# Gate weights loaded earlier, two-chunk steps, and a first tile by pieces in a two-layer encoder trunk

## The chip, the cores and the metric

The kernel runs on one core of a Trainium2 chip. The metric is the device time of one execution in microseconds (us). Before the change the median of three runs is 2396.72 us, the lowest 2395.23 and the highest 2396.8.

## The reference

A trunk of two layers works on h, the 256 tokens with 16 learned meta tokens in front: 272 rows of 2048 numbers. Each layer does the following, in float32:

```
proj = h @ w_in            # GLA q, k, v, output gate r, low-rank decay lr; NA q, k, v
g    = log_sigmoid(lr @ w_up + b_up) / 16        # for each of two directions, 4 heads x 128
o    = gla_scan(q, k, v, g_fwd) + flip(gla_scan(flip q, flip k, flip v, flip g_bwd))
o    = o * rsqrt(mean(o^2) + eps) * norm_w * silu(r)      # heads of 256 value columns
y    = neighbourhood attention of 16 heads over a 4 x 64 grid, plus the meta tokens as keys
h    = layer_norm(alpha * h + concat(o, y) @ w_out)
h    = layer_norm(alpha * h + relu(h @ w_ff1)^2 @ w_ff2)
```

w_ff1 and w_ff2 have 8192 hidden columns. The meta rows are dropped from the output, which is 256 x 2048.

## The kernel before

**Weights.** All large products use float32 split in two: a high part rounded to the fast type fp32r, and a low part, the rest. A weight tile is 128 x 1024 (512 KB): SP loads it raw (L150), ScalarE casts it to wh (L151), VectorE subtracts to get wl (L152). Each of raw, wh and wl is a ring of three buffers, and `weights` makes two tiles ahead of the one in use. TensorE runs 24 matmuls with a tile (wh with the high and the low part of x, wl with the high part; where only 256 rows are wanted, one matmul of 512 columns takes both parts of x). The activations x, y and u lie in SBUF as pairs (high, low), 16 pairs each, as places of a fixed name (y0 to y15).

**Loops.** `by_m` (L203) makes one output chunk of 128 columns after the other, with all of its weight tiles, through `eight` (L157). `by_k` (L183) keeps four accumulators (eight where `wide`) and goes through the inner chunks two at a time; it starts the kernel, where x arrives chunk by chunk (`load_x`, L304), and starts other stages whose inputs become ready one after the other. PSUM has four banks "mm" for the accumulators and four banks "bg" for everything else.

**Background work.** Everything beside the large products is written as generators whose steps are put between the weight tiles. `pump` (L105) runs so many steps of the queue fg and of the queue bg after each tile. In the queue fg of each layer stand first `gates` (L334), then for each of the eight value chunks `v_rows` (L388), which transposes a chunk of v into rows, splits it into high and low and stacks the meta rows. `gla_head` (in bg) does the attention of a head; its output is two chunks, each with seven matmuls on its own bank (L569 to L581), one step each. Each engine carries out its instructions in order, so a waiting instruction holds up all behind it on that engine; a step is put behind the newest weight split (`issue_after`, L99).

**Gates.** `gates` loads wup (98 x 1024) into a place of its own and, a step later, wlr (128 x 512) into a buffer of the raw ring; in layer 0 it also loads the constants (L339). It then casts and splits both (L345, L348 to L350), makes lr with 32 small matmuls, and does eight steps, one for each head and direction: a matmul (L368), four activations (L370, L371, L372, L374) and one VectorE operation (L373). In layer 1 it is queued after the first `by_m` and `by_k` have been written out (L263), when the places of the layer before have been closed.

**First tile.** `load_x` loads the first x chunk (L313), and `made` loads the first weight tile in pieces of 256, 256 and 512 columns; after the first piece it loads the second x chunk (L154). The 24 matmuls go through the products with wh first, then those with wl (L196).

**The end.** `ln_out` (L953) normalizes the last layer per token. It transposes the accumulated chunks into eight blocks of 128 x 512 on eight banks (`turn`), sums with matmuls against ones (L979, L983), casts the mean and its low part for a matmul that centres the blocks (L985, L986, `centre`), makes the variance (L989, L990), takes two further steps for the root (`newton`, L450 to L454), and scales each block by it with the bias added (L999 to L1002) before its output transfer (L1003).

## Time and profile before

| what | value |
|---|---|
| median of three runs | 2396.72 us |
| profiled execution, its own time | 2396.73 us |
| its span in the profile | 2394.9 us |
| TensorE busy | 2385.1 us (100%) |
| weight loads of TensorE busy | 2264.0 us (95%) |
| VectorE busy | 1539.6 us (64%) |
| ScalarE busy | 1216.7 us (51%) |
| GpSimd busy | 131.9 us (6%) |
| moved by DMA | 419.07 MB, mean 175 GB/s |
| weight splits L151, L152 | 770 of each, 1047 and 1225 ns |

How to read it: the span runs from the first to the last instruction of the profiled execution; its own time is a little longer. The page has the engines as PE and PEld (TensorE's matmuls and weight loads), ACT (ScalarE), DVE (VectorE), POOL (GpSimd) and SP (SyncE, which issues transfers here). A row of the timeline has the start, the time from the start to the end, the engine, the line, the operation with its output and inputs, the shape, how many such instructions stand in one row, and in brackets the idle time of the engine before it and what ended it. Matmuls overlap, so the time of one to the start of the next is shorter than its own. A row of the waits has who waited for whom, the sum in us, how often, and the longest. A row of windows has the stretch, its length, the busy share and number of instructions of TensorE, its weight loads, VectorE, ScalarE and GpSimd, the clock granted, the share of the DMA engines, and GB/s.

### The profile page before, as it was taken

The numbers are of one execution on the slowest core, as the hardware profiler recorded it, in microseconds if no ns is written. First come the engines' busy times: TensorE is split into PE (matmuls) and PEld (weight loads), VectorE is DVE, ScalarE is ACT, GpSimd is POOL, SyncE is SP. The second block draws the span as 40 slices with busy tenths as digits, with TensorE's granted clock in tenths as the row PEclk, the third lists the DMA queues.
The fourth block names the chain that finished last, engine by engine and source line by source line (L and its number), as shares of the span: only waits on it lengthen the run. The fifth ranks groups of instructions, "written<-read, shape, count | busy, mean of one in ns | idle before, by whom it ended". The sixth has DMA issues, their size and how long they took to land.

```text
span 2394.9 us, 43606 instructions
## 1 busy us (share of the span) xinstructions
PE 2385.1 (100%) x17666; PEld 2264.0 (95%) x17666; DVE 1539.6 (64%) x2473; ACT 1216.7 (51%) x2064; POOL 131.9 (6%) x202
## 2 busy tenths in 40 slices
PE   9999999999999999999999999999999999999999
PEld 9999999999999999999999999999988888888888
DVE  5598777775544455546576887778866445666654
ACT  5765655564433344444456766655644333444443
POOL 0021110010000000000021111100100000000000
PEclk9999999999999999999999999999999999999999
DMA  7444445555555555555556444446566555566654
GB/s 259 151 153 152 145 139 165 176 173 172 176 176 176 175 171 175 175 176 171 175 177 180 159 148 159 153 159 194 187 187 190 186 189 188 186 189 210 195 187 146
DMA packets 118073, 419.07 MB, mean 175 GB/s; under 512 B 13484, under 2 KB 14252, under 8 KB 117872
## 3 DMA queue, kind: packets, MB, share of 16 engines
q1 hardware_dynamic: 117584, 415.77, 54.9%
q8 instruction: 138, 2.26, 0.4%
q14 instruction: 63, 0.52, 0.1%
q10 hardware_dynamic: 288, 0.52, 0.1%
HBM read 414.14 MB, written 2.10 MB: 174 GB/s over the span
## 4 chain that ended last, share of the span: by engine, by line
PE 97%; DVE 1%; DMA 1%; ACT 1%; issue 0%; POOL 0%; SPq 0%; DVEq 0%; ACTq 0%; POOLq 0%
PE mm L169 35%; PE mm L172 29%; PE mm L166 23%; PE mm L199 5%; PE bg L199 1%; PE bg L504 1%; PE bg L684 1%; PE bg L633 1%; DVE wl L152 0%; PE bg L356 0%; DMA raw<-in_win 0%; PE bg L669 0%; DVE acc L913 0%; ACT wh L151 0%; POOL acc L901 0%
## 5 line engine op out<-in xcount | busy, mean ns | idle before, releaser
L152 DVE TENSOR_TENSOR wl<-raw,wh 128x1024 fp32r<-128x1024 f32 (+1 forms) x770 | 942.8, 1225 | 648.1 <-ACT wh L151 643.2
L151 ACT CAST wh<-raw 128x1024 fp32r<-128x1024 f32 (+1 forms) x770 | 805.6, 1047 | 950.7 <-PE mm L169 437.3
L169 PE MATMUL mm<-x,wh 128*128 128x272 f32 (+2 forms) x4224 | 582.0, 290 | 0.0
L169 PEld LDWEIGHTS mm<-x,wh 128*128 128x128 f32 x4224 | 548.3, 189 | 2.5 <-issue 1.1
L172 PE MATMUL mm<-x,wl 128*128 128x272 f32 (+3 forms) x3264 | 467.3, 285 | 0.0
L172 PEld LDWEIGHTS mm<-x,wl 128*128 128x128 f32 x3264 | 437.6, 188 | 13.1
L166 PE MATMUL mm<-x,wh 128*128 128x512 f32 x1152 | 294.3, 397 | 1.9 <-ACT ft L385 1.9
L166 PEld LDWEIGHTS mm<-x,wh 128*128 128x128 f32 x1152 | 207.7, 189 | 42.0 <-ACT ft L385 2.2
L172 PE MATMUL mm<-y,wl 128*128 128x272 f32 (+1 forms) x1408 | 199.5, 284 | 0.0
L172 PEld LDWEIGHTS mm<-y,wl 128*128 128x128 f32 x1408 | 188.9, 188 | 7.5
L169 PE MATMUL mm<-y,wh 128*128 128x272 f32 (+1 forms) x1440 | 195.8, 288 | 0.0
L169 PEld LDWEIGHTS mm<-y,wh 128*128 128x128 f32 x1440 | 186.1, 188 | 0.0
L166 PE MATMUL mm<-y,wh 128*128 128x512 f32 x688 | 174.1, 395 | 0.0
L172 PE MATMUL mm<-u,wl 128*128 128x272 f32 (+1 forms) x1024 | 145.3, 284 | 0.0
L166 PEld LDWEIGHTS mm<-y,wh 128*128 128x128 f32 x688 | 123.4, 188 | 22.5
L169 PE MATMUL mm<-u,wh 128*128 128x272 f32 (+1 forms) x1056 | 143.2, 288 | 0.0
L172 PEld LDWEIGHTS mm<-u,wl 128*128 128x128 f32 x1024 | 137.8, 188 | 5.6
L169 PEld LDWEIGHTS mm<-u,wh 128*128 128x128 f32 x1056 | 136.3, 188 | 0.0
L166 PE MATMUL mm<-u,wh 128*128 128x512 f32 x496 | 125.3, 395 | 0.0
L166 PEld LDWEIGHTS mm<-u,wh 128*128 128x128 f32 x496 | 89.1, 188 | 16.4
L199 PE MATMUL mm<-x,wh 128*128 128x272 f32 (+1 forms) x512 | 73.7, 289 | 0.5 <-ACT wh L151 0.4
L199 PEld LDWEIGHTS mm<-x,wh 128*128 128x128 f32 x512 | 68.0, 191 | 1.1 <-ACT wh L151 1.1
(261 smaller groups left out, 1886.4 us busy)
## 6 DMA issues: line engine op xcount, KB each, us to landing
raw<-in_wff SPq DMA_DIRECT2D x512, 512.0 KB, 3.6
raw<-in_win SPq DMA_DIRECT2D x191, 512.0 KB, 3.6
raw<-in_wout SPq DMA_DIRECT2D x64, 512.0 KB, 3.6
nb<-in_nab SPq DMA_DIRECT2D x16, 352.0 KB, 3.6
xraw<-in_xT SPq DMA_DIRECT2D x7, 272.0 KB, 5.7
out<-out SPq DMA_DIRECT2D x6, 256.0 KB, 3.0
brow<-in_norm SPq DMA_DIRECT2D x4, 256.0 KB, 5.0
wraw<-in_wup SPq DMA_DIRECT2D x2, 392.0 KB
```

The costliest lines, as they stand in the source:

```text
L151: nc.scalar.copy(wh[:, c], raw[:, c])
L152: self.wl = nc.vector.tensor_tensor(wl[:, c], raw[:, c], wh[:, c].bitcast(F32), ALU.subtract).ins
L166: mm(ps, lhsT=c(wh, j), rhs=v.both[:, :, :T], start=first and not j, stop=False)
L169: mm(ps[:, :n], lhsT=c(wh, j), rhs=v[i][:, :n], start=first and not i + j, stop=False)
L172: mm(o, lhsT=c(wl, j), rhs=h[:, :T if once else n], start=False, stop=last and j == 7)
L199: self.nc.tensor.matmul(ps[g + m][:, :n], lhsT=parts[p][0][:, c:c + P], rhs=acts[k + j][parts[p][1]][:, :n], start=k + j + p == 0, stop=k ...
L504: nc.tensor.matmul(ps[b * 64:b * 64 + 64, i * P + s * 64:i * P + s * 64 + 64], lhsT=k[:, c:c + 64], rhs=q[:, r:r + 64], start=True, stop=True)
L633: nc.tensor.matmul(ps[hh][:, t * NKEY:t * NKEY + NKEY], lhsT=q[hs, NM + t * P:NM + t * P + P], rhs=k[hs, t, :], start=True, stop=True)
L684: nc.tensor.matmul(r[hs], lhsT=(v2 if rest else v1)[:, t, hs], rhs=p2[:, t, :] if rest else p1[:, 2 * t + hh, :], start=rest, stop=not rest)
```

## The change

The change has six parts.

1. *First tile.* The second x chunk is loaded after the second piece of the weight tile instead of after the first, and the 24 matmuls of the first tile go by inner chunk and then by pairs of outputs, each pair with all three products.
2. *Gate weights.* A new function `load_gates` loads wup in two tiles of 98 x 512 and wlr in one of 128 x 512 into the places y8, y9 and y10. In layer 1 it is called when the layer begins, in layer 0 in the first step of `gates`. The cast and split of wup go in two pieces. wlr no longer takes a buffer of the raw ring.
3. *Gates.* One step does both directions of a head: two matmuls into two banks, two Abs of 272 columns, then Exp, Ln and Exp over both (544 columns), and two VectorE operations. There are four steps instead of eight in each layer.
4. *Value rows.* One generator does two chunks: six transposes in one step, then the splits and stacks of one chunk, a step's end, and those of the other.
5. *Outputs of a head.* The fourteen matmuls of both chunks are in one step.
6. *The end.* The per-token sums of the mean come before the matmul that spreads it; the mean is copied and squared by VectorE, no longer squared by ScalarE, and the variance is written ahead of mu; the first output block is scaled and sent in two halves of 256 columns, so that SP sends seven transfers instead of six.

The number of matmuls of each kind stays.

```diff
@@ -150,7 +150,7 @@
             nc.sync.dma_start(raw[:, c], ap[:, c])
             nc.scalar.copy(wh[:, c], raw[:, c])
             self.wl = nc.vector.tensor_tensor(wl[:, c], raw[:, c], wh[:, c].bitcast(F32), ALU.subtract).ins
-            if between and not p:
+            if between and p == 1:
                 between()
         return wh, wl
 
@@ -193,7 +193,7 @@
                 parts = ((wh, 0), (wh, 1), (wl, 0))
                 order = [(j, p, m) for j in range(2) for p in range(3) for m in range(4)]
                 by_output = k == nk - 2 or k == 0 and not wide
-                order.sort(key=lambda o: (by_output and o[2], o[1] // 2))
+                order.sort(key=lambda o: (o[0], o[2] // 2) if wide and not k + g else (by_output and o[2], o[1] // 2))
                 for j, p, m in order:
                     c = j * 512 + m * P
                     self.nc.tensor.matmul(ps[g + m][:, :n], lhsT=parts[p][0][:, c:c + P], rhs=acts[k + j][parts[p][1]][:, :n],
@@ -250,8 +250,9 @@
             self.vlow = [self.pair(self.yp, "y", 12 + h).both.rearrange("p a c -> p (a c)") for h in range(GH)]
             self.VS = a.tile([80, GH * GDV], F32R, name="VS", tag="VS")
             nc.gpsimd.memset(self.VS.bitcast(F32), 0.0)
-            self.y, self.gate, self.done = [None] * DC, {}, set()
+            self.y, self.gate, self.done, self.vt = [None] * DC, {}, set(), []
             if l:
+                self.load_gates()
                 self.by_m(self.x, [L + 2] * 4, lambda m, ps: self.fixed(self.ev_k, m, ps), pump=(1, NORMS[0]),
                           renew=True)
                 first = self.by_k(self.x, L, self.normed)
@@ -331,23 +332,30 @@
         for _ in range(WARM):
             self.nc.tensor.matmul(ps[:, :L], lhsT=z[:, :P], rhs=z, start=True, stop=True)
 
+    def load_gates(self):
+
+        place = lambda c: self.yp.tile([P, 2, L], F32, name=f"gw{c}", tag=f"y{c}", bufs=1).rearrange("p a c -> p (a c)")[:, :512]
+        *self.wup, self.wlr = (place(c) for c in (8, 9, 10))
+        for d, w in enumerate(self.wup):
+            self.nc.sync.dma_start(w[:LRK], self.i["wup"][self.l, :, d])
+        self.nc.sync.dma_start(self.wlr, self.i["wlr"][self.l])
+
     def gates(self):
         nc, e, l = self.nc, self.ep, self.l
-        wraw = e.tile([LRK, 2, GH * GDK], F32, name="wraw", tag="wraw")
-        nc.sync.dma_start(wraw, self.i["wup"][l])
         if l == 0:
+            self.load_gates()
             self.consts()
         yield
-        lraw = self.wp.tile([P, WB], F32, name="raw", tag="raw")[:, :512].rearrange("p (k c) -> p k c", c=32)
-        nc.sync.dma_start(lraw, self.i["wlr"][l].rearrange("p (k c) -> p k c", c=32))
         ws = e.tile([P, DC, 64], F32R, name="ws", tag="ws")
-        self.split(lraw, ws[:, :, :32], ws[:, :, 32:])
+        self.split(self.wlr.rearrange("p (k c) -> p k c", c=32), ws[:, :, :32], ws[:, :, 32:])
         yield
         uh = e.tile([LRK, 2, GH * GDK], F32R, name="uph", tag="uph")
         up = e.tile([LRK, 2, GH * GDK], F32R, name="up", tag="up")
-        nc.scalar.copy(uh, wraw)
-        nc.vector.tensor_scalar(wraw, wraw, self.sel[:, 0:1], None, ALU.mult)
-        nc.vector.scalar_tensor_tensor(up, uh.bitcast(F32), self.sel[:, 1:2], wraw, ALU.mult, ALU.add)
+        for d, w in enumerate(self.wup):
+            w = w[:LRK]
+            nc.scalar.copy(uh[:, d], w)
+            nc.vector.tensor_scalar(w, w, self.sel[:, 0:1], None, ALU.mult)
+            nc.vector.scalar_tensor_tensor(up[:, d], uh[:, d].bitcast(F32), self.sel[:, 1:2], w, ALU.mult, ALU.add)
         ps = self.bank()
         o = ps[:, :L]
         for k in range(DC):
@@ -363,16 +371,17 @@
         self.stack(t, lr, 32, (0, 64), 32)
         yield
         for h in range(GH):
+            z = [self.bank()[:, :L] for _ in range(2)]
+            g = e.tile([P, 2, L], F32, name="gt", tag="gt", bufs=2)
             for d in range(2):
-                z = self.bank()[:, :L]
-                nc.tensor.matmul(z, lhsT=up[:, d, h * GDK:h * GDK + GDK], rhs=lr, start=True, stop=True)
-                g = e.tile([P, L], F32, name="gt", tag="gt", bufs=2)
-                nc.scalar.activation(g, z, AF.Abs)
-                nc.scalar.activation(g, g, AF.Exp, scale=-1.0)
-                nc.scalar.activation(g, g, AF.Ln, bias=self.one)
-                nc.vector.scalar_tensor_tensor(g, z, 0.0, g, ALU.min, ALU.subtract)
-                nc.scalar.activation(self.decay[h][:, d, :], g, AF.Exp, scale=1 / TAU)
-                yield
+                nc.tensor.matmul(z[d], lhsT=up[:, d, h * GDK:h * GDK + GDK], rhs=lr, start=True, stop=True)
+                nc.scalar.activation(g[:, d], z[d], AF.Abs)
+            nc.scalar.activation(g, g, AF.Exp, scale=-1.0)
+            nc.scalar.activation(g, g, AF.Ln, bias=self.one)
+            for d in range(2):
+                nc.vector.scalar_tensor_tensor(g[:, d], z[d], 0.0, g[:, d], ALU.min, ALU.subtract)
+            nc.scalar.activation(self.decay[h], g, AF.Exp, scale=1 / TAU)
+            yield
 
     def ev_q(self, m, ps):
         self.nc.scalar.mul(self.qk[m][:, 1, :self.n], ps, GDK ** -0.5)
@@ -383,20 +392,23 @@
     def ev_v(self, c, ps):
         vt = self.ep.tile([P, L], F32, name="ft", tag="ft", bufs=4)
         self.nc.scalar.copy(vt, ps)
-        self.fg.append(self.v_rows(c, vt))
-
-    def v_rows(self, c, vt):
+        self.vt.append(vt)
+        if c % 2:
+            self.fg.append(self.v_rows(c // 2, self.vt[-2:]))
+
+    def v_rows(self, h, vt):
+
         nc = self.nc
         yield
-        pt = self.bank()
+        pt = [self.bank() for _ in range(2)]
         for i in range(3):
             n = P if i < 2 else NM
-            nc.tensor.transpose(pt[:n, i * P:i * P + P], vt[:, i * P:i * P + n], self.ident)
-        o = slice(c * P, c * P + P)
-        low = self.vlow[c // 2][:, c % 2 * T:c % 2 * T + T]
-        self.split(pt[:, :T], self.V[:, c].rearrange("p i c -> p (i c)"), low)
-        self.stack(pt[:NM, T:T + P], self.VS[:, o], NM, (0, 32), 64)
-        yield
+            for e in range(2):
+                nc.tensor.transpose(pt[e][:n, i * P:i * P + P], vt[e][:, i * P:i * P + n], self.ident)
+        for e in range(2):
+            self.split(pt[e][:, :T], self.V[:, 2 * h + e].rearrange("p i c -> p (i c)"), self.vlow[h][:, e * T:e * T + T])
+            self.stack(pt[e][:NM, T:T + P], self.VS[:, h * GDV + e * P:h * GDV + e * P + P], NM, (0, 32), 64)
+            yield
 
     def ev_na(self, j, ps):
 
@@ -578,7 +590,7 @@
             nc.tensor.matmul(o, lhsT=self.VS[:, c], rhs=am, start=False, stop=True)
             nc.scalar.activation((rs, tn)[e], o, AF.Square)
             os_.append(o)
-            yield
+        yield
         nc.vector.tensor_tensor(rs, rs, tn, ALU.add)
         ms = yield from self.mean(rs, GDV, pool=g2)
         self.newton(rs, ms, self.eps, tn)
@@ -976,18 +988,23 @@
 
         turn(0), turn(1)
         p1, ms = self.bank()[:, :T], self.bank()
-        nc.tensor.matmul(p1, lhsT=one, rhs=self.s1, start=True, stop=True)
-        for k, s in enumerate((self.s1, self.s2)):
+
+        def per_token(s, k):
             for h in range(2):
                 c = 2 * k + h
                 nc.tensor.matmul(ms[:, c:c + 1], lhsT=s[:, h * P:h * P + P], rhs=one[:, :1], start=True, stop=True)
+
+        per_token(self.s1, 0)
+        nc.tensor.matmul(p1, lhsT=one, rhs=self.s1, start=True, stop=True)
+        per_token(self.s2, 1)
+        var, rs, tn, mean = (t(nm, [P, 2]) for nm in ("var2", "rs2", "tn2", "mean2"))
+        nc.vector.tensor_copy(mean, ms[:, 0:2])
+        nc.vector.tensor_tensor(tn, mean, mean, ALU.mult)
+        nc.vector.tensor_tensor(var, ms[:, 2:4], tn, ALU.subtract)
         mu = t("mu", [96, T], F32R)
         nc.scalar.copy(mu, p1[:96])
         nc.vector.tensor_tensor(mu[32:64], p1[32:64], mu[32:64].bitcast(F32), ALU.subtract)
         turn(2)
-        var, rs, tn = (t(nm, [P, 2]) for nm in ("var2", "rs2", "tn2"))
-        nc.scalar.activation(tn, ms[:, 0:2], AF.Square)
-        nc.vector.tensor_tensor(var, ms[:, 2:4], tn, ALU.subtract)
         centre(0), centre(1), centre(2)
         for i in range(3, 8):
             turn(i), centre(i)
@@ -998,9 +1015,11 @@
                 queue = nc.scalar
                 nc.scalar.activation(o, bank[i], AF.Identity, scale=f)
                 nc.gpsimd.tensor_tensor(o, o, b, ALU.add)
-            else:
-                nc.vector.scalar_tensor_tensor(o, bank[i], f, b, ALU.mult, ALU.add)
-            queue.dma_start(self.out[h * P:h * P + P, g * 512:g * 512 + 512], o)
+            parts = [(0, T), (T, 512)] if i == 0 else [(0, 512)]
+            for c in map(lambda p: slice(*p), parts):
+                if i not in (1, 3):
+                    nc.vector.scalar_tensor_tensor(o[:, c], bank[i][:, c], f, b[:, c], ALU.mult, ALU.add)
+                queue.dma_start(self.out[h * P:h * P + P, g * 512 + c.start:g * 512 + c.stop], o[:, c])
 
 
 def layout(inputs):
```

## Prediction

> **What bounds the kernel now.** I read the page's busy times first, then the waits, and last the timeline around each place where TensorE waits.
>
> ```profile
> span 2394.9 us, 43606 instructions
> ...
> PE 2385.1 (100%) x17666; PEld 2264.0 (95%) x17666; DVE 1539.6 (64%) x2473; ACT 1216.7 (51%) x2064; POOL 131.9 (6%) x202
> ```
>
> TensorE is busy for the whole span but 9.8 us, so only three things can move the time: the matmuls that it runs (their number stays), the few places where it waits, and the two ends, where it has nothing to do. The waits name one place that this change touches.
>
> ```profile
> ACT wh L151 <- PE mm L169: 437.3, 251, 3.1
> ...
> ACT uph L348 <- DMA wraw<-in_wup: 3.8, 2, 3.5
> ...
> PE mm L166 <- ACT ft L385: 1.9, 1, 1.9
> ```
>
> The first line says that ScalarE's casts of weights mostly wait for TensorE to give a tile back: the stream runs ahead. The third is the only long wait of TensorE between the ends, one wait; the second is behind it. The timeline there (SP, ScalarE, TensorE):
>
> ```profile
> 1274.69 0.34 SPq L337 DMA_DIRECT2D wraw<-in_wup  x1
> 1276.34 0.34 SPq L342 DMA_DIRECT2D raw<-in_wlr  x1
> ...
> 1280.14 1.04 ACT L348 CAST uph<-wraw 98x1024 fp32r<-98x1024 f32 x1 [3.49 <-DMA wraw<-in_wup]
> 1281.09 0.38 ACT L385 COPY ft<-mm 128x272 f32<-128x272 f32 x1
> ...
> 1279.17 0.41 PE L199 MATMUL mm<-x,wl 128*128 128x272 f32 x2
> 1281.52 2.14 PE L166 MATMUL mm<-x,wh 128*128 128x512 f32 x8 [1.93 <-ACT ft L385]
> ```
>
> In layer 1 SP issues the gates' weights only at 1274.69. ScalarE reaches the cast (uph) at once and stands idle for 3.49 us; behind it in the same queue stands ft, which empties the four mm banks, and TensorE needs one of them. Two weight matmuls from 1279.17 end near 1279.42, and the next starts at 1281.52: 2.1 us are lost.
>
> **The change, part by part. Gates' weights sooner, layer 1.** The three loads now go out at the start of the layer, into the places of y8 to y10, whose last readers are the matmuls of the layer before.
>
> ```profile
> 1216.71 12.38 SPq L150 DMA_DIRECT2D raw<-in_win  x5
> ...
> 1223.22 1.16 PE L172 MATMUL mm<-y,wl 128*128 128x272 f32 x8
> ```
>
> The last of those readers runs from 1223.22, so the places are free near 1224.4, while SP is inside a row of five weight loads that takes it 12.38 us. The loads stand on SP ahead of the fourth; it can be held up by three issues of about 0.33 us (the rows of SP above), about 1 us, which the two tiles in hand (3 us each) cover; without that cover the 1 us would be TensorE's. They then land some 45 us before uph needs them. On ScalarE, uph (1.04, now in two pieces) and the split of wlr then wait for nothing. The four accumulators end in turn, six matmuls (0.76 us) apart: the last at 1279.42, so the first at 1277.15; its eviction (ft, 0.38), even behind a weight cast and a piece of uph, is done by about 1278.0, ahead of 1279.42. What is late next on ScalarE is the cast of the next weight tile behind the other three evictions; the tiles in hand cover it. wlr also leaves its slot of the weight ring (the row at 1276.34 stood ahead of a weight load). I take the whole 2.1 us: **-2.1**. Ends: 0, if another wait stands at the same place, and -2.1.
>
> **First tile by pieces.**
>
> ```profile
> 4.10 1.11 PE L199 MATMUL mm<-x,wh 128*128 128x272 f32 x4
> ...
> 4.75 0.42 ACT L221 CAST x<-xraw 128x272 fp32r<-128x272 f32 x1 [0.97 <-DMA xraw<-in_xT]
> 5.18 0.40 ACT L151 CAST wh<-raw 128x256 fp32r<-128x256 f32 x1
> ...
> 5.63 2.58 PE L199 MATMUL mm<-x,wh 128*128 128x272 f32 x12 [0.43 <-ACT wh L151]
> ...
> 6.27 0.62 ACT L151 CAST wh<-raw 128x512 fp32r<-128x512 f32 x1 [0.69 <-DMA raw<-in_win]
> 6.92 0.69 DVE L152 TENSOR_TENSOR wl<-raw,wh 128x512 fp32r<-128x512 f32 x1 [0.88 <-ACT wh L151]
> ...
> 7.57 1.05 ACT L151 CAST wh<-raw 128x1024 fp32r<-128x1024 f32 x1 [0.69 <-DMA raw<-in_win]
> ...
> 8.05 1.17 PE L199 MATMUL mm<-x,wl 128*128 128x272 f32 x8
> ```
>
> The second piece of weights is now loaded one place ahead of the second x chunk, so its cast comes at about 4.65 instead of 5.18 (it trades places with the x cast), done by 5.05. In the new order the first six matmuls need the first piece alone; at the early pace (12 matmuls of 5.63 and 4 of 4.10 give about 0.23 each) they run from 4.10 to 5.5, and the six after them to 6.8, with no gap. Then the third piece decides, whose load keeps its place: cast done at 6.89, low part at 7.61. Four matmuls run to 7.4, wait 0.2, and eight at 0.126 (8 in about 1.01 us, from later rows of the same kind) end near 8.65. Before, eight low matmuls from 8.05 end at 9.06. The gain is 0.4. It is capped there: the next tile's cast (7.57) ends at 8.62.
>
> Whether the 0.4 lasts depends on the stream in the next 30 us, into which layer 0 also moves wlr (256 KB) and two more issues on SP.
>
> ```profile
> 33.08 1.01 SPq L317 DMA_DIRECT2D xraw<-in_xT  x1
> ...
> 35.35 0.74 ACT L221 CAST x<-xraw 128x272 fp32r<-128x272 f32 x2 [0.93 <-DMA xraw<-in_xT]
> ...
> 36.28 1.93 PE L199 MATMUL mm<-x,wh 128*128 128x272 f32 x14
> ```
>
> The high half of that x chunk is there at about 35.75 and TensorE starts at 36.28: 0.5 us in hand, of which 0.4 goes to the gain itself. If the loads ahead make it 1 us later (a 512 KB tile takes 3.6 us from issue to landing by the page, half of it is wlr), 0.9 is lost; if the gap in the transfers before takes it up, nothing. Ends 0 and +1.0; I take +0.1, near the lower end, because wlr only moves from 35.71 to an earlier, emptier stretch. Net head: **-0.3**.
>
> **Both gates of a head, value rows of two chunks, both outputs in one burst.** The number of matmuls stays. What a burst costs beside its matmuls:
>
> ```profile
> 69.83 1.18 PE L172 MATMUL mm<-x,wl 128*128 128x272 f32 x8
> 70.84 0.29 PE L368 MATMUL bg<-lr,up 98*128 98x272 f32 x1
> 70.97 2.18 PE L169 MATMUL mm<-x,wh 128*128 128x272 f32 x16
> ...
> 71.85 0.39 ACT L370 ACTIVATE gt<-bg 128x272 f32<-128x272 f32 x1
> ...
> 105.60 0.49 PE L394 MATMUL bg<-ident,ft 128*128 128x128 f32 x3
> 105.84 2.26 PE L169 MATMUL mm<-x,wh 128*128 128x272 f32 x16
> ```
>
> Start to start, a weight matmul takes (70.84-69.83)/8 = 0.126 us and the gate's 0.13: an interruption costs its own matmul and nothing else. Three transposes take 0.24, again no more than the matmuls beside them. So 24 fewer interruptions (four each of gates, value rows and outputs in either layer) save TensorE at most 0.1 us. On the other side, the last value rows now put transposes of chunk 7 behind only three of chunk 6 and a weight matmul (about 0.45 us) after chunk 7's eviction, where the transposes of chunks 4 to 6 stood before. That eviction takes 0.38 (ft above), 0.6 with a start and an end around it: a wait of 0.1 to 0.2 in each layer. Ends -0.1 and +0.5, **+0.2** taken, the middle. What hides the rest is the tiles in hand.
>
> ScalarE's share of a gate step, from the groups of shapes between 60 and 115 us:
>
> ```profile
> L372 ACT ACTIVATE gt<-gt,one 128x272 f32<-128x272 f32 x8 | 4.2, 523 | 0.3
> ...
> L371 ACT ACTIVATE gt<-gt 128x272 f32<-128x272 f32 x8 | 3.5, 432 | 0.3
> L370 ACT ACTIVATE gt<-bg 128x272 f32<-128x272 f32 x8 | 3.1, 385 | 0.0
> ...
> L527 ACT COPY S<-qk 128x544 f32<-128x544 f32 x1 | 0.7, 651 | 0.0
> ```
>
> A copy of 544 takes 0.651 and one of 272 (ft at 1281.09) takes 0.38, so doubling the width adds 0.27. A step of two directions is two Abs (0.385 each) and Exp, Ln and the second Exp (taken like the first) at about 0.70, 0.79, 0.70: 2.96 us; with a cast of 1.04 some 4.0 against a tile of 3.28 (24 weight matmuls at 0.126 and two of the gates). ScalarE falls behind by 0.7 us in each of four steps, 2.1 at the fourth, less than the one to two tiles that its casts are ahead; then it catches up. Cost 0 under that cover; without it, up to 2.1 in each layer.
>
> The Trainium skill (Perfetto Trace Analysis, Optimizing Scalar/DVE Operations) says that grouping into larger operations helps throughput if the engine is saturated, and that breaking up instructions may finish work sooner where ScalarE or VectorE aren't saturated but cause bubbles elsewhere. The trace has ScalarE at 51%, so by that rule the grouping earns nothing, as in the sum, and the second half speaks for the slower rival below; no run yet shows it.
>
> **The end.**
>
> ```profile
> 2384.18 0.42 DVE L986 TENSOR_TENSOR mu<-bg,mu 32x256 fp32r<-32x256 f32 x1 [0.74 <-ACT mu L985]
> ...
> 2384.56 0.17 ACT L989 ACTIVATE tn<-bg 128x2 f32<-128x2 f32 x1 [0.42 <-PE bg L983]
> 2384.77 0.16 DVE L990 TENSOR_TENSOR var<-bg,tn 128x2 f32<-128x2 f32 x1 [0.17 <-ACT tn L989]
> ...
> 2386.25 1.41 DVE L1002 SCALAR_TENSOR_TENSOR out<-mm,rs,brow 128x512 f32<-128x512 f32 x2
> ...
> 2387.03 3.86 SPq L1003 DMA_DIRECT2D out<-out  x6
> ...
> 2388.00:2389.00 1.00, 0.98 (x7) 0.59 (x5) 1.00 (x3) 0.00 (x0) 1.00 (x2) 1.00 1.02 381
> ```
>
> After the last sums (about 2384.53) one ScalarE and one VectorE operation lead to var. The change makes it three on VectorE, copy, product, difference (0.16 to 0.2 each), and the low part of mu (0.42) can stand between them, since it is ready at the same moment; the variance is then 0.1 (without mu) to 0.5 later, and the outputs with it. The first output goes out in halves: 0.42 instead of 0.74 until its first transfer, 0.3 back. From 2388 on the transfers run at 381 GB/s with all engines busy (share 1.02), so the end follows the first issues: 0.5-0.3 = +0.2, and a little for twice the rows in block 0 and 0.1 more on VectorE. Ends -0.2 and +0.6; **+0.3** taken, toward the upper, since mu is ready first.
>
> The Trainium skill (Perfetto Trace Analysis, DMA Optimizations) has a rule on either side: transfers under 2 KB carry significant overhead, and splitting may let some start sooner while engines are idle. By the second alone the end would be 0.3 earlier than by the first; the trace shows saturation from 2388 on and no run here shows a 1 KB row's overhead yet.
>
> **The sum.** The profiled execution took 2396.73 us, 1.8 over its span and 0.01 over the median of the runs shown, 2396.72. 2396.73 - 2.1 - 0.3 + 0.2 + 0.3 = 2394.8.
>
> **The rivals.**
> *The stall is paid again.* The wait at 1279 goes, but what was gained is given back within the next tiles, by x at 35.35 arriving 1 us late (+0.9), the value rows at their upper end (+0.3 more) and the end at its upper end (+0.3), or another wait of ScalarE stands at 1279: 2396.3 to 2396.9. For it speaks that the x chunk has only 0.5 us in hand; against it that the layer 1 loads have 45.
> *ScalarE's lag holds PSUM banks.* This is the slower one. Four banks serve the background work. A gate step now takes two, given back when both operations of VectorE have read them. From the rows above: two Abs, two wide operations (2.26 us) and two of VectorE, 0.4 to 0.45 each for 272 columns (the mu row has 0.42 for 256), make about 3.2 us after the first Abs, which starts 1.0 behind the gate's matmul (70.84, 71.85). Two steps later (6.6 us) the same banks are wanted: 2.4 in hand for the third step, and with the lag growing by 0.7 a step 1.7, 1.0 and 0.3 at the three reuses behind it, the value rows last. A wait of TensorE there lets ScalarE catch up, so a layer pays the largest shortfall once. If a step lags by 0.33 us more than reckoned (1.3 over four), each layer pays 1.0 and the kernel is as slow as before; with 0.9 more (3.6), 3.3 a layer, 6.6 in both: 2401.4; with more, later. For it: 0.3 us is thin. Against it: the casts of weights, over a fourth of ScalarE's load in these steps, can wait, the stream being ahead.
> *Each interruption costs more than its rows show.* If every one of the 24 hid 0.2 us that comes back elsewhere (weight loads, evictions), the gain is 4.8 more: 2390. The starts above speak against it.
>
> **How the numbers follow.** About 0.2% (4.8 us) is what a measurement of this kernel can tell from no change: 2391.9 to 2401.5. The forecast has 0.59 (its own range 2393.2 with all lower ends to 2396.2), paid again 0.14, banks 0.20 (0.11 of it over 2401.5, the rest between 2396.7 and that), interruptions 0.07. The range runs from 2393.0 to 2400.5 and leaves out the interruptions and about 0.12 of the banks. Faster by over 0.2%: 0.07; slower: 0.11; within: 0.82.
>
> **What would show it.** Right: no wait of TensorE for ft near 1279, uph without idle time for its load, first low matmuls of tile one done near 8.65, the groups of L166 without idle. Wrong: rows of TensorE waiting for ACT or DVE behind gates or value rows (banks), an idle before the x cast of k = 10 longer than before, the first output issue later than 2387.03 plus 0.3, seen from the last weight matmul.

## The result, and the profile after

The changed kernel takes 2390.93 us (2389.38 to 2392.44, 13 runs) against 2396.72 us (2394.83 to 2397.8, 13 runs): the ratio is 0.9975 with a 95% interval of 0.9967 to 0.9982. That is 5.8 us less where 1.9 less was forecast, and below the range, which began at 2393.0.

The page of the changed kernel: span, busy times, and the group of the matmuls of layer 1 that waited before.

```profile
span 2388.8 us, 43610 instructions
...
PE 2378.8 (100%) x17666; PEld 2260.5 (95%) x17666; DVE 1539.1 (64%) x2480; ACT 1214.0 (51%) x2041; POOL 130.4 (5%) x202
...
L166 PE MATMUL mm<-x,wh 128*128 128x512 f32 x1152 | 294.1, 397 | 0.0
```

TensorE runs the same 17,666 matmuls in 2378.8 busy us instead of 2385.1. The wait of 1.9 us in the group of L166 is gone. But the span has lost 6.1 us and the busy time 6.3; the idle time is 0.2 longer, because in this profile the head waits 2.3 us for weight casts where it waited 0.4, and the end is longer. This is the first thing to see: what looked like a floor, TensorE busy from end to end, has come down.

The place of the stall in the timeline of the changed kernel (SP, ScalarE, TensorE):

```profile
1221.68 0.77 SPq L340 DMA_DIRECT2D gw<-in_wup  x2
1222.49 0.37 SPq L341 DMA_DIRECT2D gw<-in_wlr  x1
...
1273.61 1.14 ACT L356 CAST uph<-gw 98x512 fp32r<-98x512 f32 x2
...
1275.60 0.37 ACT L394 COPY ft<-mm 128x272 f32<-128x272 f32 x1
...
1277.22 0.41 PE L199 MATMUL mm<-x,wl 128*128 128x272 f32 x2
1277.47 2.02 PE L166 MATMUL mm<-x,wh 128*128 128x512 f32 x8
```

The loads are issued 51 us before the cast that needs them, which no longer idles for them; the first eviction is ready before the last of the four accumulators ends, and the next matmul follows after 0.25 us for two, with no gap.

The rest is found only by laying the two traces over each other, weight matmul by weight matmul (both run the same 16,096 in the same order apart from the first 24). Worked out from the starts of their rows in the two profiles, changed minus before:

| stretch (time before) | difference, us |
|---|---|
| head, to the gates' first burst (56 us) | +1.0 |
| gates to neighbourhood attention, layer 0 (56 to 346) | -0.6 |
| wout, layer 0 (371 to 456) | +0.6 |
| wff2, first half, layer 0 (650 to 855) | -1.5 |
| wff2, second half, layer 0 (1037 to 1230) | -1.4 |
| the stall (1279) | -2.1 |
| gates to neighbourhood attention, layer 1 (1282 to 1616) | -1.1 |
| the rest of layer 1 (1616 to 2382) | -1.6 |
| after the last weight matmul | +0.6 |

Two of these rows belong to this one profile of the kernel before: against a second one (below), wout differs by 0.0 instead of +0.6 and the second half of wff2 by -0.2 instead of -1.4. The others remain: stages without a wait and without a changed instruction have become faster. In the timeline, three successive weight tiles of wff2 in the kernel before:

```profile
701.56 2.17 PE L169 MATMUL mm<-y,wh 128*128 128x272 f32 x16
...
704.57 2.17 PE L169 MATMUL mm<-u,wh 128*128 128x272 f32 x16
...
707.58 2.17 PE L169 MATMUL mm<-u,wh 128*128 128x272 f32 x16
```

and in the changed one:

```profile
702.17 2.15 PE L169 MATMUL mm<-y,wh 128*128 128x272 f32 x16
...
705.14 2.16 PE L169 MATMUL mm<-u,wh 128*128 128x272 f32 x16
...
708.13 2.16 PE L169 MATMUL mm<-u,wh 128*128 128x272 f32 x16
```

A tile of 24 matmuls takes 3.01 us before, each time; after, 2.97 to 2.99. The windows view counts the same thing. Its columns here are the stretch, its length, TensorE's busy time and matmuls, the clock, the share of the DMA engines, and GB/s. First before, then after:

```profile
660.00:820.00 160.00, 160.00 (x1277) 1.00 0.55 176
```

```profile
660.00:820.00 160.00, 160.00 (x1286) 1.00 0.58 178
```

TensorE is busy for 160.00 of 160 us in both, at the same clock, and does nine matmuls more. The Trainium skill (Perfetto Trace Analysis, Identifying the Most-Contended Engine) says that TensorE's matmul busy share does not measure how close it is to its best, because pipelined matmuls look smaller in the trace. These two rows agree that it does not; the reason is another here, since the share stands at its top in both.

### The profile page after: what moved, and what is told of

It is laid out like the page before. It is cut to its first block, busy times and chain, and to the rows that moved or that the text cites. A ratio compares the mean times of both kernels' runs of the same rounds, so it can differ in the third digit from the quotient of the medians.

```text
span 2388.8 us, 43610 instructions
## 1 busy us (share of the span) xinstructions
PE 2378.8 (100%) x17666; PEld 2260.5 (95%) x17666; DVE 1539.1 (64%) x2480; ACT 1214.0 (51%) x2041; POOL 130.4 (5%) x202
## 4 chain that ended last, share of the span: by engine, by line
PE 99%; DVE 0%; DMA 0%; ACT 0%; SPq 0%; issue 0%; DVEq 0%; ACTq 0%
PE mm L169 35%; PE mm L172 29%; PE mm L166 23%; PE mm L199 6%; PE bg L199 1%; PE bg L516 1%; PE bg L696 1%; PE bg L645 1%; PE bg L364 0%; PE bg L681 0%; PE bg L823 0%; DMA raw<-in_win 0%; PE bg L407 0%; PE bg L558 0%; PE bg L586 0%; PE bg L587 0%
## 5 line engine op out<-in xcount | busy, mean ns | idle before, releaser
L172 PEld LDWEIGHTS mm<-x,wl 128*128 128x128 f32 x3264 | 437.6, 188 | 13.2
L166 PE MATMUL mm<-x,wh 128*128 128x512 f32 x1152 | 294.1, 397 | 0.0
L166 PEld LDWEIGHTS mm<-x,wh 128*128 128x128 f32 x1152 | 207.7, 189 | 39.8 <-issue 0.8
L166 PE MATMUL mm<-y,wh 128*128 128x512 f32 x688 | 172.5, 392 | 0.0
L166 PEld LDWEIGHTS mm<-y,wh 128*128 128x128 f32 x688 | 123.1, 188 | 21.3
L166 PE MATMUL mm<-u,wh 128*128 128x512 f32 x496 | 125.3, 395 | 0.0
L166 PEld LDWEIGHTS mm<-u,wh 128*128 128x128 f32 x496 | 89.1, 188 | 16.4
```

Source lines behind the costliest of these rows:

```text
L166: mm(ps, lhsT=c(wh, j), rhs=v.both[:, :, :T], start=first and not j, stop=False)
L172: mm(o, lhsT=c(wl, j), rhs=h[:, :T if once else n], start=False, stop=last and j == 7)
```

## The experiments

Only y0 to y10 differ in address between the operands of the weight matmuls of the two kernels (beside the order within the first tile): the gate loads ask for y8, y9 and y10 first, so the pool gives them the first three places, and y0 to y7 move up by three places of 2,176 bytes. The theory for the first four runs was that this, unasked for, is the greater part of the gain (theory P); the rivals were the altered steps, and the stall alone. The medians of all runs, each beside runs of the kernel before on the same chip:

| run | median, us | before beside it | ratio, 95% interval |
|---|---|---|---|
| places of the change alone | 2393.2 | 2397.09 | 0.9987 (0.9978 to 0.9996) |
| changed kernel, old places | 2394.14 | 2397.09 | 0.9988 (0.9980 to 0.9997) |
| gate loads alone, old places | 2395.39 | 2397.09 | 0.9993 (0.9984 to 1.0002) |
| steps alone | 2395.73 | 2397.09 | 0.9995 (0.9986 to 1.0003) |
| first tile alone | 2396.27 | 2397.09 | 0.9998 (0.9989 to 1.0007) |
| end alone | 2397.59 | 2397.09 | 1.0002 (0.9993 to 1.0011) |
| y8 first (one place up) | 2393.09 | 2397.09 | 0.9984 (0.9976 to 0.9993) |
| y8, y9 first (two places up) | 2396.2 | 2397.09 | 0.9997 (0.9988 to 1.0006) |
| changed, old end | 2389.66 | 2397.39 | 0.9968 (0.9955 to 0.9980) |
| changed, variance ahead of mu | 2390.17 | 2397.39 | 0.9970 (0.9958 to 0.9981) |
| changed, late wlr in layer 0 | 2390.48 | 2397.39 | 0.9971 (0.9960 to 0.9983) |
| x pairs of 280 columns | 2393.83 | 2397.39 | 0.9985 (0.9976 to 0.9994) |
| u16 to u23 swapped | 2393.62 | 2396.73 | 0.9987 (0.9978 to 0.9996) |
| x0 to x7 swapped | 2396.5 | 2396.73 | 1.0000 (0.9991 to 1.0008) |
| changed, old end, x of 280 | 2388.63 | 2396.73 | 0.9967 (0.9954 to 0.9979) |
| kernel before again | 2396.76 | 2396.73 | 1.0001 (0.9990 to 1.0011) |

An interval is about 2 us to either side, so the sizes of single parts are read from the profiles as well. The mean time from one weight matmul to the next, in ns, worked out from the first and last start of the same 624, 1248, 1464 and 1392 matmuls of layer 0:

| kernel | wout (y) | wff2, first half (y, u) | wff2, second half | wff1, second half (x) |
|---|---|---|---|---|
| before | 125.43 | 125.56 | 125.90 | 126.11 |
| before again | 126.34 | 125.56 | 125.11 | 126.11 |
| changed | 126.29 | 124.58 | 124.98 | 126.11 |
| places of the change alone | 126.30 | 124.58 | 124.98 | 126.11 |
| changed, old places | 126.36 | 125.56 | 125.11 | 126.11 |
| gate loads alone; steps alone | 126.34; 126.36 | 125.56 | 125.11 | 126.11 |
| one place up | 126.30 | 124.58 | 124.98 | 126.11 |
| two places up | 125.48 | 125.56 | 125.09 | 126.11 |
| u16 to u23 swapped | 126.34 | 124.59 | 125.04 | 126.11 |
| x0 to x7 swapped | 126.36 | 125.56 | 125.11 | 126.11 |
| x pairs of 280 columns | 126.34 | 124.44 | 124.80 | 126.11 |

**The places alone.**

```diff
             self.vlow = [...]
+            for c in (8, 9, 10) if l == 0 else ():
+                self.pair(self.yp, "y", c)
```

> Kernel before with y8, y9 and y10 given the first places of the pool of pairs, as the new gate loads give them; y0 to y7 move up by three places (6,528 bytes), nothing else changes. Theory P (places): outside the ends and the one stall, the changed kernel's matmuls follow one another about 1 ns closer in the stages that read y and u (wff2: 125.6 to 124.6 ns on the mean), and 1 ns less close in wout of layer 0; this comes from the new places alone. Then this run is 4.3 us faster than before, 2392.4, wff2 of layer 0 gains 2.9 us and wout of layer 0 loses 0.6. Rival S (steps): the spacing follows from the altered bursts and their times; then this run stays within 0.5 us of before.

Measured: 3.9 us less on the medians. The windows row of this run has the count of the changed kernel:

```profile
660.00:820.00 160.00, 160.00 (x1286) 1.00 0.57 176
```

No instruction differs; only addresses do. Theory P holds for the greater part of the gain. One expectation in it does not: the loss in wout of layer 0 is not from the places, as the second profile of the kernel before shows (126.34 there, 125.43 in the first).

**The changed kernel with the old places.**

```diff
+            for c in range(12) if l == 0 else ():
+                self.pair(self.yp, "y", c)
```

> Changed kernel with y0 to y11 in the places they had before; the gate loads still go early, into y8 to y10. Theory P: it loses the 4.3 us and takes about 2395.2, with the spacing of before in wff2 (125.6 ns). Rival S: it keeps the spacing and takes about 2390.9.

Measured: 2394.14, 2.95 us under the kernel before beside it, so some 3 us of the 5.8 are lost, with the spacing of before:

```profile
660.00:820.00 160.00, 160.00 (x1276) 1.00 0.57 175
```

It lies 1.1 below what theory P named, 2395.2: by these medians the other parts together are worth 2.95 and not 1.5 to 1.9, though an interval of 2 us holds both.

**The gate loads alone**, `load_gates` with its calls and the copies in two pieces put into the kernel before, with y0 to y11 kept where they were.

```diff
             if l:
+                self.load_gates()
...
-        nc.scalar.copy(uh, wraw)
+        for d, w in enumerate(self.wup):
+            w = w[:LRK]
+            nc.scalar.copy(uh[:, d], w)
```

> Kernel before with the early gate loads alone, y0 to y11 in the places of before, eight gate steps as before. My prediction: the wait at 1279 goes and nothing else moves: 2.1 us faster, 2394.6. Rival (another wait takes its place): 2396.7. Theory P expects no change of spacing in wff2.

Measured: 1.7 less, with an interval that just holds nothing. In its profile the wait at 1279 is gone, and no other stands there. In layer 0 two new waits show (waits view of this run):

```profile
PE mm L199 <- ACT x L221: 0.6, 1, 0.6
...
PE mm L199 <- DVE x L222: 0.5, 1, 0.5
```

These are the x chunk near 36 us, 1.1 us together, at the upper end of my bound for the early wlr (+1.0). That the early wlr makes it late is not shown: the profile with y8 and y9 first, whose wlr is late as before, has the same two waits, and two for weights beside them, while the changed kernel's, with the early wlr, has neither. From the waits view of the run with y8 and y9 first:

```profile
PE mm L199 <- ACT x L221: 0.4, 1, 0.4
...
PE mm L199 <- DVE x L222: 0.4, 1, 0.4
```

**The steps alone**: gates, value rows and outputs as in the change.

```diff
-            for d in range(2):
-                z = self.bank()[:, :L]
...
+            z = [self.bank()[:, :L] for _ in range(2)]
...
-            yield
+        yield
         nc.vector.tensor_tensor(rs, rs, tn, ALU.add)
```

> Kernel before with both gates of a head in a step, value rows of two chunks and both outputs of a head in one burst; loads, places, first tile and end as before. My prediction: +0.2 us. Theory P with the traces read burst by burst: fewer bursts (97 instead of 119 in the two stretches) give 0.6 us a layer, 1.3 faster, 2395.4, the spacing in wff2 as before. Rival S: 4 to 6 us faster, 2391 to 2393.

Measured: 1.4 less on the medians, where 0.2 more was forecast. The interval holds both and nothing as well, so the traces have to decide. A burst is the background matmuls that stand between two weight matmuls. From the last weight matmul ahead of the gates' bursts (56 us) to the end of the neighbourhood attention (353), layer 0 takes 0.5 to 0.6 us less than in the two profiles of the kernel before; the same stretch of layer 1 (1282 to 1616) takes 0.9 less. That is 1.4 to 1.5 together with 22 bursts fewer, 0.06 to 0.07 us for each. It does not come from the gates' bursts, which add 0.13 alone and 0.26 as a pair. Which of the others brings it is open: in layer 0 a burst of 40 matmuls of a head and one of 20 of the neighbourhood attention add 1.59 and 1.19 apart and 2.58 together, but the seven other pairs of kinds that now stand together add about 0.1 more than apart, and six transposes in a burst add 0.57 where two bursts of three added 0.48.

**The first tile and the end alone** (the diffs of these parts as in the change).

> Kernel before with the first tile by pieces alone. My prediction: -0.4 us for the head by itself, 2396.7 from the 2397.1 that before took beside the first four runs. Rival (landing times of the first loads, which differed by 2.8 us from run to run in the profiles so far, decide and not the order): no change within 0.5 us on the median. A third: the parts so far add up to 7.0 us against 5.8 of the whole change, so this part and the end may cost 1.1 together: +0.5 here.

> Kernel before with the changed end alone. My prediction: +0.3 us, with ends -0.2 and +0.6. In the profile the stretch from the last weight matmul to the span's end grows by that; the changed kernel's grew by 0.58. Rival (the halves start the transfers earlier and that decides): -0.2 or less.

Measured: 0.8 less and 0.5 more, both within their intervals of nothing. The profiles tell more. The second tile starts at 9.06 to 11.20 us in eleven profiles with the old first tile (mean 9.97), and at 8.36 to 10.24 in seven with the new one (mean 9.38). So the new order is some 0.6 earlier on the mean, less than the spread of either. The third expectation, that this part costs 0.5, finds no support, though the interval does not exclude it. The end, from the last weight matmul's start to the span's end, is 13.86 us here, 13.74 in the changed kernel and 13.0 to 13.2 in those with the old end (13.15 and 13.18 in the two of the kernel before): 0.6 to 0.7 more, the upper end of my bound.

**One place and two places up.**

```diff
+            for c in (8,) if l == 0 else ():      # one place; (8, 9) for two
+                self.pair(self.yp, "y", c)
```

> Kernel before with y8 alone in the first place: y0 to y7 move up by one place, 2,176 bytes. A place is 8.5 times 256 bytes, so every place by an odd number further swaps which of neighbouring pairs starts at 64 and which at 192 beyond a multiple of 256; three places (the changed kernel) and one place do this to y0 to y7 alike, and y8 to y15 keep theirs. Theory A (offset within 256 bytes): 3 to 4 us faster, 2393.3 to 2394, with wff2 of layer 0 at 124.6 ns. Rival B (the distance from other tiles, or the region): something else, or nothing.

> Kernel before with y8 and y9 in the first places: y0 to y7 move up by two places, 4,352 bytes, 17 times 256, so every pair keeps its offset within 256 bytes. Theory A (offset within 256 bytes): as before within 0.5 us, wff2 of layer 0 at 125.6 ns. Rival B (the distance or the region): a gain between none and that of three places, some 2.6 us if it grows with the distance.

Measured: one place 4.0 less, two places 0.9 less with an interval that holds nothing. The rows of one place and of two:

```profile
660.00:820.00 160.00, 160.00 (x1287) 1.00 0.58 177
```

```profile
660.00:820.00 160.00, 160.00 (x1277) 1.00 0.58 176
```

One place and three gain 4, two gain nothing that is clear of the interval: it is not the distance, but its being odd or even. Theory A, the start within 256 bytes, is the one that passes here; a place is 8.5 times 256 bytes.

**u swapped instead of y.** Neighbours of u16 to u23 change places, and y stays.

```diff
-                u = [self.pair(self.yp, "y", k) if k < DC else self.pair(up, "u", k) for k in range(2 * DC)]
+                swap = sorted(range(2 * DC), key=lambda k: k ^ (DC <= k < 24))
+                u = {k: self.pair(self.yp, "y", k) if k < DC else self.pair(up, "u", k) for k in swap}
+                u = [u[k] for k in range(2 * DC)]
```

> Kernel before with u16 to u23 in swapped places, neighbour with neighbour, so that their starts within 256 bytes alternate 192, 64 instead of 64, 192; y stays. Theory A (the regular alternation over all tiles of a stage holds TensorE in a slow round, and any tile that breaks it frees it): wff2 of layer 0 goes from 125.56 ns a matmul to about 124.6 and the run is 2.5 to 4 us faster. Rival (y's places themselves, for what reads or writes them): 125.56 and no change.

Measured: 3.1 less, and the same count:

```profile
660.00:820.00 160.00, 160.00 (x1286) 1.00 0.57 175
```

So it is nothing particular to y or to its places. In the kernel before, the eight operands of every tile of wff2 begin at 64 and 192 beyond a multiple of 256 bytes in turn, and every tile then has the same times to 0.1 ns. One tile of the four with 192 and 64 in turn, whichever it is, breaks this: in the changed kernel the tile of y0 to y7 takes 125.5 ns a matmul, that of y8 to y15 124.0, those of u 124.4, though these three lie where they lay. With u swapped the pattern moves along: the tile of u16 to u23 takes 125.5, the one behind it 124.0, the other two 124.4 to 124.5. Each tile's spacing depends on what went before it.

**x swapped, and x at another distance.**

```diff
-        w = L + 2 if name == "x" else L
+        w = 280 if name == "x" else L
```

```diff
+            if k < 8 and not c:
+                self.pair(self.xp, "x", k + 1)
             self.x[k + c] = h, lo = self.pair(self.xp, "x", k + c)
```

> Kernel before with pairs of x 2,240 bytes apart (280 columns) instead of 2,192 (274): the starts of their high parts become multiples of 64 bytes, as those of y and u are, instead of multiples of 16; y and u keep their offset within 256 bytes. Theory A, widened (the spacing follows from the starts of the moving operands): the stages that read x, at 126.1 ns a matmul, come to about 125 or below; at 1 ns for the 5,300 matmuls of layer 0 that is 5 us faster, 2392. Rival (only y's places matter, x's spacing has another cause): no change within 0.5 us.

> Kernel before with x0 to x7 in swapped places, neighbour with neighbour. The stages that read x took 126.11 ns a matmul with two different distances of x, to the hundredth. Theory A by the letter: a tile that breaks the regular order frees this round too, 125 or below, 3 to 5 us faster. Rival (the round of x's stages is held by something else, as the equal 126.11 at two distances suggests): 126.11, no change within 0.5 us.

The distance of x pairs in the kernel before is 2,208 bytes, not 2,192 as the expectation had it, so their starts were multiples of 32. Swapping did nothing (0.2 us less), and neither run moved the second half of wff1, which reads x, from 126.11 ns: what holds that figure is open. The run with 280 columns gained 3.6 us all the same. In its profile, against the second one of the kernel before, 1.0 of it lies in the stretches from the gates to the neighbourhood attention (0.4 in layer 0, 0.6 in layer 1), which read x; ahead of the gates, too, the matmuls that read x run at 125.63 instead of 126.04 ns. The greater part, 2.2, lies in wff2, which does not read x at all:

```profile
660.00:820.00 160.00, 160.00 (x1288) 1.00 0.58 177
```

That went against both theories. There y, u and the weights move by 512 bytes, which leaves their starts within 256 alone, and yet all tiles of wff2's first half take 124.4 to 124.5. So the regular alternation does not by itself hold a tile at 125.5. Taken with the tiles of u above, it fits that a stage keeps a rhythm which depends on how it was entered; it was not shown. In the last stages of layer 1 this kernel does not gain (170.52 ns over 4,000 matmuls of 256 to 512 columns, 170.54 before), where the changed one (170.22), one place up (170.22) and swapped u (170.19) do.

**The kernel before once more.**

> The kernel before once more, for its profile. If the spacing belongs to the program, its stages take the same times as in the first profile (wout of layer 0 125.43, wff2 125.56 and 125.90 ns, x's stages 126.11), and the head alone differs; if it differs from run to run, one of them is off by 0.5 ns or more.

Measured: 2396.76. Two of the four stages repeat to the hundredth (125.56 and 126.11), two take another value (wout 126.34 for 125.43, wff2's second half 125.11 for 125.90: tiles of 124.5 for 125.5). The same program's second half in its first profile and in its second:

```profile
1045.00:1205.00 160.00, 160.00 (x1274) 1.00 0.55 175
```

```profile
1045.00:1205.00 160.00, 160.00 (x1282) 1.00 0.56 176
```

So some stages have two rhythms and differ from run to run, by 0.6 us in wout and 1.2 in wff2's second half, and the head differs by 1.5 (71.0 and 72.5 us at the 481st weight matmul). wff2's first half has no such pair: it takes 125.56 in all nine profiles that keep the starts of before and x's distance, and 124.6 in all eight with one tile's starts the other way round. Among the other runs that keep the starts of before within 256 bytes and x's distance, all have one of the two values, within 0.05 ns, in either stage. The rest of layer 1 varies too: with no y or u moved it takes 0.65 us longer in the profile of the gate loads alone and 0.5 longer in that of x0 to x7 swapped. The stall, too, was not always 2.1: in eleven profiles with the late gate loads it is 0.9 to 2.1, 1.5 on the mean.

**The changed kernel, three parts taken back or mended.** The old end; the low part of mu put behind the variance; wlr of layer 0 loaded a step later.

```diff
-        nc.vector.tensor_tensor(var, ms[:, 2:4], tn, ALU.subtract)
+        end = nc.vector.tensor_tensor(var, ms[:, 2:4], tn, ALU.subtract).ins
...
-        nc.vector.tensor_tensor(mu[32:64], p1[32:64], mu[32:64].bitcast(F32), ALU.subtract)
+        with self.tc.issue_after(end):
+            nc.vector.tensor_tensor(mu[32:64], p1[32:64], mu[32:64].bitcast(F32), ALU.subtract)
```

> Changed kernel with the end of before. The profiles put the end (last weight matmul to the span's end) at 13.0 to 13.2 us with the old end and 13.7 to 13.9 with the new one. So 0.6 us less than the changed kernel, 2390.3 where that takes 2390.9. Rival: the new end saves elsewhere what it costs here, no change.

> Changed kernel with the low part of mu put behind the variance on VectorE. My prediction's step: mu's low part (0.42 us) standing before the variance is what makes the new end late, and the halves of the first block would give 0.3 back. Then the end falls from 13.7 to about 13.2 to 13.3 us, 2390.4. Rival (the centring matmuls wait for mu and become the last): no change, 13.7.

> Changed kernel with wlr of layer 0 loaded a step later, as before; layer 1 stays early. In the run with the gate loads alone TensorE waited 1.1 us more for the x chunks near 36 us, as the upper end of my bound for the early wlr had it. By that 0.5 to 1.2 us less than the changed kernel, 2389.7 to 2390.4. Rival (the first 70 us are decided by landing times that differ from run to run): no change within 0.5.

Measured: 2389.66, 2390.17 and 2390.48. The changed kernel did not run beside them; against the kernel before beside them they gain 7.7, 7.2 and 6.9, where the changed kernel gained 5.8 in its own measurement, and intervals of 2 to 3 us do not tell these apart. The ends in the profiles are 13.07, 13.28 and 13.74 us. The timeline of the changed kernel, and then of the one with the variance ahead, shows the step:

```profile
2378.27 0.42 DVE L1006 TENSOR_TENSOR mu<-bg,mu 32x256 fp32r<-32x256 f32 x1
2378.72 0.16 DVE L1003 TENSOR_TENSOR var<-bg,tn 128x2 f32<-128x2 f32 x1
...
2380.72 4.70 SPq L1022 DMA_DIRECT2D out<-out  x7
```

```profile
2378.26 0.16 DVE L1003 TENSOR_TENSOR var<-bg,tn 128x2 f32<-128x2 f32 x1
2378.45 0.42 DVE L1007 TENSOR_TENSOR mu<-bg,mu 32x256 fp32r<-32x256 f32 x1
```

With the order turned round the variance comes 0.46 earlier and the end is as much shorter, still 0.1 to 0.2 over the old one. Late wlr in layer 0 gains nothing beyond its interval, and its profile reaches the 481st weight matmul at 72.29 us where the changed kernel's does at 72.33: in these two profiles, both with a late head, the early wlr costs nothing.

**The best put together**: the changed kernel with the old end and x pairs of 280 columns.

> Changed kernel with the end of before and the pairs of x at 280 columns. Where both gains are the same stages freed from the same round, nothing is added: 2389.5 to 2390, as with the old end alone. Where they have causes of their own, they add up: 2386 to 2387.

Measured: 2388.63, 8.1 us under the kernel before; 1.0 under the changed kernel with the old end, which ran on another chip, where the kernel before was 0.7 slower; their intervals overlap. It lies between the two forecasts, and the profiles say why: in wff2 the two gains are one and the same (its first half runs at 124.58), while the stretches from the gates to the neighbourhood attention are 1.0 shorter than with the old end alone.

## Why the prediction was wrong

**The step that failed** is the first one: "only three things can move the time: the matmuls that it runs (their number stays), the few places where it waits, and the two ends". It took the time of a matmul as given once their number stays. Between the two kernels it is not: in the stages that read y and u it falls from 125.56 to 124.58 ns and the like, 3.3 us in all against the second profile of the kernel before (1.5 and 0.2 in wff2 of layer 0, 1.6 in the end of layer 1), 3 to 4 us on the medians of three runs that change nothing but places. The step "into the places of y8 to y10" was costed for its waits only. That asking for these places first moves eight other tiles was not seen, though it follows from the diff. The range could not have held this: its own lower ends add up to 2393.9 (the prediction has 2393.2), and nothing in it stood for a faster matmul. That the rival with costlier interruptions named 2390, close to the measured time, is luck: it puts 4.8 on interruptions, which the runs have at 1.4 to 1.5.

**Gate loads, -2.1**: right in mechanism. The wait is gone and none took its place; the profile used had the longest stall of eleven, whose mean is 1.5, so this term was worth 1.5.

**Head, -0.3**: the order gains some 0.6 at the second tile over many profiles. The waits at the x chunk near 36 us, 0 to 1.1 in the profiles with the early wlr, can take that away again, but they also come without it. In the changed kernel's own profile the head was 0.9 later at the second tile, since the second tile's weights came late:

```profile
4.09 0.74 PE L199 MATMUL mm<-x,wh 128*128 128x272 f32 x4
...
6.96 1.03 PE L199 MATMUL mm<-x,wh 128*128 128x272 f32 x6 [1.12 <-ACT wh L151]
...
9.93 0.52 PE L199 MATMUL bg<-x,wh 128*128 128x272 f32 x2 [1.18 <-ACT wh L151]
```

The pace at the start, 0.23 a matmul, was taken from one profile and does not repeat. The trace's record of TensorE's granted clock begins at 6.65 us in the first profile of the kernel before, at 10.34 in the second and at 4.24 in the changed kernel's; matmuls without a wait start 0.227 us apart ahead of that moment and 0.126 behind it, and over all profiles it lies between 4.2 and 10.6 us. Here the twelve matmuls that need the first two pieces have started by 5.55, and TensorE waits for the third piece, as the working had it, until 6.96. The first tile's last matmul starts at 8.45 (the second of two from 8.33) and ends near 8.7, where 8.65 was forecast.

**Steps, +0.2**: wrong. "an interruption costs its own matmul and nothing else" holds for the single matmuls of the gates that were looked at, not for all bursts: the stretches with them are 1.4 to 1.5 us shorter, and the medians 1.4. The rival with 0.2 us for each of 24 interruptions had the sign, at about a third of its price.

The waits expected among the steps were there and small. The last value rows in the timeline of the changed kernel:

```profile
110.92 0.49 PE L407 MATMUL bg<-ident,ft 128*128 128x128 f32 x3
...
111.55 0.55 PE L407 MATMUL bg<-ident,ft 128*128 128x128 f32 x3
```

From the first to the fourth transpose there are 0.63 us; three transposes (0.24) and the weight matmul between (0.13) make 0.37 and not the 0.45 of the working, so the wait is 0.26, a little over the forecast 0.1 to 0.2. The slower rival, banks held by ScalarE's lag, did not come: a step's ScalarE work is 2 x 0.389 + 0.659 + 0.750 + 0.650 = 2.84 us by the groups of shapes (two of its rows follow), against 2.96 reckoned, and no matmul waits for a gate.

```profile
L380 ACT ACTIVATE gt<-gt,one 128x544 f32<-128x544 f32 x4 | 3.0, 750 | 0.2
L378 ACT ACTIVATE gt<-bg 128x272 f32<-128x272 f32 x8 | 2.7, 389 | 0.0
```

**End, +0.3**: right in mechanism, at the upper end of its bound, 0.6 (0.4 of it at the first output transfer: 5.61 us after the last weight matmul's start instead of 5.25; the variance is 0.63 later where up to 0.5 was reckoned).

Summed with the measured sizes against the second profile of the kernel before: places -3.3, stretches with the steps -1.5, stall -1.7 (with the matmuls right behind it), head up to the gates -0.5, end +0.6: 6.4 in all against 6.5 between the spans.

## What to carry to other kernels

A TensorE that is busy all the time is not at its floor: count its matmuls in equal windows of two profiles before taking their time as fixed. Any change that allocates tiles in another order moves the operands of matmuls that it doesn't touch, so compare addresses along with instructions, and try an order or a pad on purpose, which adds no instruction. Take a second profile of the same kernel before putting a price on a single stall or on the first microseconds; here the two differed by 0.5 us in the stall and by 1.5 in the head.

## What was not expected of the hardware

In stages of back-to-back matmuls of 272 columns in fp32r, the spacing takes one of a few values that repeat to a few hundredths of a nanosecond between runs and kernels (124.58, 125.11, 125.56, 126.11). Which of them depends on the starts of the moving operands within 256 bytes (one place up against two, 9 to 10 matmuls in 160 us) and also on more than the operands of the stage itself: u's tiles speed up when y's move, and wff2 when x's distance changes. Why, and why the second half of wff1 stays at 126.11 whatever was tried, is open. Two runs of one program differ in two of four stages. The moment at which the pace of the first matmuls goes from 0.227 to 0.126 us differs from run to run, by 6.3 us over the profiles here.
